# First loads and u products in a fixed order, first weights split on the chip, scores on two row halves, shorter inverse roots

## The chip, the cores and the metric

One core of a Trainium2 chip runs the kernel. The metric is the time of one execution on the device in microseconds (us), taken as the median of several runs. Engines: PE multiplies matrices, ACT applies functions and casts, DVE does arithmetic on tiles, POOL does simple arithmetic and issues some DMAs, SP only issues DMAs. Each engine works off its own instruction queue in order.

## The reference

A sequence of 512 rows of 1024 numbers passes two blocks. All in fp32:

```
# block 1
proj = rmsnorm(x) @ w_in                       # q, k, v, u, gates
o = softmax(q0 k0) v - lam softmax(q1 k1) v    # 8 heads, two 64-wide halves each, causal
s = s5_layer(u)                                # state space: tables from exp/sin/cos, a scan, gelu, glu
h = x + (g_attn * (o @ w_attn_proj) + g_ssm * (s @ w_ssm_proj)) @ w_out
h = h + (silu(conv gate) * conv val) @ w_down  # from rmsnorm(h) @ w_up
# block 2
m = [dilated_attention(8 heads of 64), rg_lru(...)] @ w_out_2
x = h + rms_norm(m);  x = x + rms_norm(relu(rms_norm(x) @ w_ff_in_2)^2 @ w_ff_out_2)
```

## The kernel before, in words

**Products.** Every fp32 operand a is split into hi, a rounded copy, and lo = a - hi. A product is three matmuls: hi by hi, hi by lo, lo by hi, all added up in PSUM (`mm3`). Activations are split by one cast on ACT and one subtraction on DVE (`split` of `Net`; tiles hi and lo, 128x512).

**Weights.** A `Unit` is a 512 KB piece of a weight matrix. `dma` issues its load into one of RB = 2 buffers raw (SP's queue). `split` casts raw to whi on ACT, writes wlo = -whi on ACT, and issues on POOL's queue a DMA that reads the weight from HBM a second time and adds it into wlo. There are WB = 4 buffers each of whi and wlo. After the split the unit gives raw back (`self.raw = None`). `drive` goes through the list of steps, and ahead of each it issues splits for units up to WB ahead and loads up to RB beyond that; `dma` returns at once if the unit holds a raw buffer.

**The order.** The program is a list of steps with costs. `merge` interleaves lists in proportion to cost. The build system then sets the order of instructions on each engine by readiness and program order, except where program order is kept by request.

**The front.** `front` loads cols (the small parameters), eight x tiles of 256 KB, two of the four u units (512 KB each), ident, pmask, and two spi tiles of 256 KB (the state space parameters), all on SP. For each x tile: hi and lo with the gain, then its square on ACT, and POOL adds the squares. `u_steps` multiplies x by the four u units into four PSUM banks, 96 matmuls of 128x512, position s by position s; `row1` sums the squares over the channels (tile rn, eight matmuls with one column) and takes the inverse root on DVE (`rsqrt`: 12 operations on a few columns). Beside it `ssm_steps` makes the tables of the state space: parameters (exp, sin; tiles sp, pw, rot), rotations ec and es (products by doubling, quarters 0 and 2 on one engine and the others on the other, POOL and DVE), and for each quarter Q the weights G, CL, L, whose products and transposes on PE (tile ps) give GT and K. Then U (u transposed), S = U by GT on PE, the scan on DVE, and xs, the states turned back, three operations on DVE and three on POOL. `gate_steps` multiply x by the gate units (PSUM tile cm, 24 matmuls a unit, then a product ga with R on DVE). `front2` loads the mask, the rope tables and gg (the head gains); POOL makes tab from rope and gg. `attention` joins these lists: u and two gate steps merged with the first part of the tables, then the rest.

**The attentions.** In the first attention a step of 64-row halves c = 0, 1 makes two score tiles s, each by three matmuls on 64 partitions, c = 0 first. In the second attention (`attn2_steps`) each step makes the scores of one head and one query tile (128, 256, 384 or 512 keys); heads 2j and 2j+1 lie on partitions 0 to 63 and 64 to 127 of the same tiles, and head 2j+1 comes four steps after head 2j's first. Following steps normalise (DVE), transpose (tile ta) and multiply with v (tile o).

Every engine call goes through a wrapper, so that nearly all instructions carry line 122; one goes by the names of the tiles.

Of the kernel before, what the change touches and what calls it, by code (L numbers as in the profile page):

```python
# [112 lines left out]
class Engine:  # L113


    def __init__(self, eng):
        self.eng = eng

    def __getattr__(self, name):
        f = getattr(self.eng, name)  # L120
        u = lambda a: a.ap if isinstance(a, V) else a
        return lambda *a, **k: f(*(u(x) for x in a), **{n: u(x) for n, x in k.items()})  # L122


class Core:
    def __init__(self, nc):
        for n in ("vector", "scalar", "gpsimd", "tensor", "sync"):
            setattr(self, n, Engine(getattr(nc, n)))


class Unit:


    def __init__(self, net, src, a, b):
        self.net, self.src, self.a, self.b = net, src, a, b
        self.pool = False
        self.raw = None
# [10 lines left out]
    def split(self):  # L148
        n = self.net
        w = self.a * self.b  # L150
        hi = n.wp.tile([128, 1024], F32R, tag="whi", bufs=n.WB, name=n.nm("whi"))
        lo = n.wp.tile([128, 1024], F32R, tag="wlo", bufs=n.WB, name=n.nm("wlo"))
        raw = self.raw[:, :w]
        n.nc.scalar.copy(out=hi[:, :w], in_=raw)
        n.nc.scalar.activation(out=lo[:, :w], in_=hi[:, :w].bitcast(F32), func=AF.Copy, scale=-1.0)
        self.raw = None
        self.hi = hi[:, :w].rearrange("p (a b) -> p a b", a=self.a)
        self.lo = lo[:, :w].rearrange("p (a b) -> p a b", a=self.a)

        n.nc.gpsimd.dma_start(out=self.lo, in_=self.src, accum_op=ADD)  # L160
# [23 lines left out]
class Net:  # L184
# [8 lines left out]
    def __init__(self, tc, ctx, ins, out):  # L193
        self.nc, self.I, self.out = Core(tc.nc), ins, out
# [80 lines left out]
    def front(self):  # L275
# [3 lines left out]
        self.u_units = [self.wunit("w_in_u", 0, 2 * u, 2) for u in range(4)]  # L279
        cols = self.c([128, NCOLS], "cols")  # L280
        Q.dma_start(out=cols, in_=I["cols"])
# [12 lines left out]
        self.ones1 = self.c([128, 128], "ones1")  # L294
        V.memset(self.ones1, 1.0)
        self.xg = []
        for k in range(8):
            x = self.t("x")
            Q.dma_start(out=x, in_=I["xT"][128 * k : 128 * k + 128, :])
            if k in (1, 3):  # L300
                self.u_units[k // 2].dma()
            self.xg.append(self.split(x, scale=self.cols["norm1_gain"][:, k : k + 1]))
            S.activation(out=x, in_=x, func=AF.Square)
            if k == 0:
                acc = x
            else:
                G.tensor_add(out=acc, in0=acc, in1=x)
        Q.dma_start(out=self.ident, in_=I["ident"])
        Q.dma_start(out=self.pmask, in_=I["pmask"])
        self.sp_in = [self.t("spi") for _ in range(2)]  # L310
        for i in range(2):
            Q.dma_start(out=self.sp_in[i], in_=I["ssmp"][:, 512 * i : 512 * i + 512])
        self.acc = {"x": acc}

    def row1(self):
# [3 lines left out]
        acc = self.acc.pop("x")  # L319
        ps = self.ps("rn")  # L320
        for j in range(8):
            a = acc[:, 128 * j : 128 * j + 128] if j < 4 else acc[:, j - 4 : 512 : 4]
            nc.tensor.matmul(ps[:, j : j + 1], a, self.onesd, start=True, stop=True)
# [9 lines left out]
        self.R1 = self.t("R1")  # L333
        S.copy(out=self.R1, in_=self.spread(rs))
# [35 lines left out]
    def rsqrt(self, out, x, w):  # L370

        V = self.nc.vector
        f, t, h = self.sm(w), self.sm(w), self.sm(w)
        V.tensor_copy(out=f, in_=x.bitcast(I32))
        V.tensor_scalar(out=f, in0=f, scalar1=-0.5, scalar2=1597463007.0, op0=MUL, op1=ADD)
        y = self.sm(w)
        V.tensor_copy(out=y.bitcast(I32), in_=f)

        V.tensor_mul(out=h, in0=y, in1=x)
        for i in range(2):  # L380
            V.scalar_tensor_tensor(out=t, in0=y, scalar=-0.5, in1=h, op0=MUL, op1=MUL)
            V.scalar_tensor_tensor(out=y, in0=t, scalar=1.5, in1=y, op0=ADD, op1=MUL)
            if i == 0:
                V.scalar_tensor_tensor(out=h, in0=t, scalar=1.5, in1=h, op0=ADD, op1=MUL)
        V.tensor_mul(out=h, in0=y, in1=x)
        V.scalar_tensor_tensor(out=t, in0=y, scalar=-0.5, in1=h, op0=MUL, op1=MUL)
        V.scalar_tensor_tensor(out=out, in0=t, scalar=1.5, in1=y, op0=ADD, op1=MUL)
# [50 lines left out]
    def qkv_steps(self, g):  # L438
# [4 lines left out]
        for kind, base in (("q", 0), ("k", 4), ("v", 8)):  # L443
            st = {"ps": [None, None], "y": [None, None]}
            units = [self.wunit("w_in_qkv", base + g, 4 * u, 4) for u in range(2)]
            for u, un in enumerate(units):
                un.pool = u == 0 or kind == "v"
# [98 lines left out]
    def attn_steps(self):  # L546
# [6 lines left out]
        def scores(u):  # L553
# [8 lines left out]
            mx = self.sm(2)  # L562
            for c in range(2):
                cs = slice(64 * c, 64 * c + 64)
                (qh, ql), (kh, kl) = grp["q"][hl], grp["k"][hl]
                ps = self.ps("s")
                self.mm3(ps[:, :n], (qh[cs, qs], ql[cs, qs]), (kh[cs, :n], kl[cs, :n]), True, True)
# [118 lines left out]
    def attention(self):  # L686
# [23 lines left out]
    def u_steps(self):  # L710
# [6 lines left out]
        for ui, un in enumerate(units):  # L717
            for b in range(2):
                def fn(ui=ui, un=un, b=b):
                    for s in (2 * b, 2 * b + 1):  # L720
                        if ui == 0:
                            st[s] = self.ps("u")
                        for kk in range(2):
                            k = 2 * ui + kk
                            xh, xl = self.xg[k]
                            sl = slice(s, 512, 4)
                            wh, wl = un.hi[:, kk, :], un.lo[:, kk, :]
                            mm = nc.tensor.matmul
                            mm(st[s], xh[:, sl], wh, start=k == 0, stop=False)
                            mm(st[s], xh[:, sl], wl, start=False, stop=False)  # L730
                            mm(st[s], xl[:, sl], wh, start=False, stop=k == 7)
                        if ui == 3:
                            if s == 0:
                                self.Z = [self.t("z") for _ in range(4)]
                            for q in range(4):
                                z = self.Z[q].rearrange("p (g s c) -> p g s c", g=8, s=4)[:, :, s, :]
                                src = st[s][:, q * 128 : q * 128 + 128].rearrange("p (g c) -> p g c", c=16)
                                S.activation(out=z, in_=src, func=AF.Copy, scale=self.rsp[:, s : s + 1])
                steps.append(Step(2.6, fn, un))
# [234 lines left out]
    def ssm_states(self, Q):  # L974
# [523 lines left out]
    def attn2_steps(self, q, k, att):  # L1498
# [3 lines left out]
        units = [(h, qt) for h in range(8) for qt in (3, 2, 1, 0)]  # L1502
        st = {}

        def scores(u):
            h, qt = u
            n = (qt + 1) * 128
            qs = slice(qt * 128, qt * 128 + 128)
            cs = slice(64 * (h % 2), 64 * (h % 2) + 64)
            (qh, ql), (kh, kl) = q[h // 2], k[h // 2]  # L1510
            ps = self.ps("s")
            self.mm3(ps[:, :n], (qh[cs, qs], ql[cs, qs]), (kh[cs, :n], kl[cs, :n]), True, True)
            e = self.t("e")
            mx, sm = self.sm(1), self.sm(1)
            V.tensor_tensor_reduce(out=e[:, :n], in0=ps[:, :n], in1=self.dmask[:, 512 - n :], scale=1.0,
# [4 lines left out]
            if h % 2 == 1 and qt == 0:  # L1520
                q[h // 2] = k[h // 2] = None
# [7 lines left out]
        def turn(u):  # L1529
# [7 lines left out]
            if qt % 2 == 1:  # L1537
                st["aT"] = [[self.tr("aT").rearrange("p (k q) -> p k q", k=2) for _ in range(2)] for _ in range(pr + 1)]
            for v in range(pr + 1):
                w = min(2, nk - 2 * v)  # L1540
                hi, lo = (a[:, :w, (qt % 2) * 128 : (qt % 2) * 128 + 128] for a in st["aT"][v])
                self.split(ps[:, 256 * v : 256 * v + w * 128].rearrange("p (k q) -> p k q", q=128), hi=hi, lo=lo)
            if qt % 2 == 0:
                st["pv", h, qt // 2] = st.pop("aT")
# [38 lines left out]
    def ffn2(self):  # L1583
# [29 lines left out]
        for f, un in first:  # L1613
            un.pool = True
# [152 lines left out]
```

## Time and profile before

| | us |
|---|---|
| median of 3 runs (1492.16 to 1494.91) | 1493.3 |
| profiled execution | 1495.94 |
| its span on the core | 1494.2 |
| PE busy | 1435.4 |
| DVE busy | 701.0 |
| ACT busy | 844.4 |
| POOL busy | 338.3 |

The span runs from the first to the last instruction. Busy times of PE are modelled ends of a pipeline: issue to issue is the better measure for one matmul. In the rows, "out<-in" names the tiles, and a bracket at the end of a row gives the idle time before it and what ended it.

### The profile page before, as it was taken

What the parts mean: (1) busy time and instruction counts of PE and PEld (TensorE: products, weight loads), DVE (VectorE), ACT (ScalarE), POOL (GpSimd) and SP (SyncE); (2) the same over time, 40 slices, a digit from 0 to 9 for tenths busy, and PEclk for the clock granted to TensorE, in tenths of its full rate; (3) what the DMA queues carried; (4) which work ended last, traced back from release to release, by engine and by line L of the source; (5) the groups of instructions that cost most, each with busy time, mean ns of one, the idle gap of its engine ahead of it and who ended that gap; (6) DMA issues with size and microseconds to landing.
All of it is one profiled execution on the core that took longest, in us unless ns stands there. A gap on an engine that the chain in (4) does not pass through costs nothing.

```text
span 1494.2 us, 20260 instructions
## 1 busy us (share of the span) xinstructions
PE 1435.4 (96%) x7448; PEld 1214.1 (81%) x7448; DVE 701.0 (47%) x1928; ACT 844.4 (57%) x1329; POOL 338.3 (23%) x450
## 2 busy tenths in 40 slices
PE   4898999999999999999999999999998999999997
PEld 4787898998888888888888887777887888888886
DVE  5977867877643345555541114565446111120003
ACT  6755466667544566666654445866556555454333
POOL 4763312212101211111121222103122111111110
PEclk9999999999999999999999999999999999999999
DMA  8564465555679878888889887756265888988994
GB/s 243 128 141 93 107 155 131 122 116 127 141 186 193 189 180 198 193 193 194 194 186 206 195 197 173 167 115 142 58 140 120 193 193 190 193 192 191 197 195 98
DMA packets 70451, 245.28 MB, mean 164 GB/s; under 512 B 8016, under 2 KB 8656, under 8 KB 70352
## 3 DMA queue, kind: packets, MB, share of 16 engines
q0 software_dynamic: 32912, 118.50, 48.4%
q1 hardware_dynamic: 36864, 124.43, 24.8%
q8 instruction: 59, 0.97, 0.3%
q10 hardware_dynamic: 576, 1.05, 0.2%
q14 instruction: 40, 0.33, 0.1%
HBM read 241.85 MB, written 2.10 MB: 163 GB/s over the span
## 4 chain that ended last, share of the span: by engine, by line
PE 78%; DVE 13%; ACT 3%; issue 2%; DMA 2%; POOL 1%; SPq 0%; DVEq 0%; ACTq 0%; POOLq 0%
PE cm L122 54%; PE ff L122 11%; PE pj L122 4%; DVE s L122 3%; PE s L122 2%; PE o L122 2%; PE v L122 1%; PE ta L122 1%; PE ps L122 1%; DVE e L122 1%; DVE v L122 1%; DVE lo L122 1%; DMA wlo<-in_w_ff_in_dram 1%; DVE oc L122 1%; ACT e L122 1%
## 5 line engine op out<-in xcount | busy, mean ns | idle before, releaser
L122 PE MATMUL cm<-hi,whi 128*128 128x512 f32 (+1 forms) x1328 | 513.1, 387 | 2.5 <-ACT hi L122 2.5
L122 PE MATMUL cm<-hi,wlo 128*128 128x512 f32 (+1 forms) x1328 | 509.7, 384 | 2.5 <-DMA wlo<-in_w_ff_in_dram 2.5
L122 PE MATMUL cm<-lo,whi 128*128 128x512 f32 (+1 forms) x1328 | 509.8, 384 | 2.2 <-DVE lo L122 2.1
L122 ACT CAST whi<-raw 128x1024 fp32r<-128x1024 f32 (+1 forms) x226 | 235.6, 1043 | 410.6 <-PE cm L122 320.8
L122 PEld LDWEIGHTS cm<-hi,wlo 128*128 128x128 f32 x1328 | 251.5, 189 | 51.5 <-ACT p L122 2.5
L122 PEld LDWEIGHTS cm<-lo,whi 128*128 128x128 f32 x1328 | 251.7, 190 | 51.0 <-DVE lo L122 3.7
L122 PEld LDWEIGHTS cm<-hi,whi 128*128 128x128 f32 x1328 | 251.3, 190 | 51.0 <-ACT hi L122 3.1
L122 ACT ACTIVATE wlo<-whi 128x1024 fp32r<-128x1024 f32 (+1 forms) x226 | 236.0, 1045 | 2.4
L122 PE MATMUL pj<-whi,hi 128*128 128x256 f32 x384 | 111.6, 291 | 0.0
L122 PE MATMUL pj<-wlo,hi 128*128 128x256 f32 x384 | 108.8, 283 | 0.0
L122 PE MATMUL pj<-whi,lo 128*128 128x256 f32 x384 | 108.7, 283 | 0.0
L122 PE MATMUL ff<-wlo,hi 128*128 128x512 f32 x256 | 99.7, 389 | 1.0 <-DMA wlo<-in_w_ff_out_dram 1.0
L122 PE MATMUL ff<-whi,hi 128*128 128x512 f32 x256 | 99.6, 389 | 0.0
L122 PE MATMUL ff<-whi,lo 128*128 128x512 f32 x256 | 99.6, 389 | 0.0
L122 DVE SCALAR_TENSOR_TENSOR y<-z,cols,y 128x511 f32<-128x511 f32 (+2 forms) x100 | 75.1, 751 | 46.1 <-ACT y L122 44.3
L122 POOL DMA_DIRECT2D wlo<-in_w_up_dram x44 | 37.8, 858 | 203.4 <-ACT wlo L122 203.4
L122 DVE SCALAR_TENSOR_TENSOR p<-cm,R 128x512 f32<-128x512 f32 (+1 forms) x35 | 22.2, 644 | 113.6 <-PE cm L122 112.3
L122 PEld LDWEIGHTS pj<-whi,hi 128*128 128x128 f32 x384 | 73.8, 192 | 0.9 <-issue 0.6
L122 PEld LDWEIGHTS pj<-wlo,hi 128*128 128x128 f32 x384 | 73.9, 192 | 0.1
L122 PEld LDWEIGHTS pj<-whi,lo 128*128 128x128 f32 x384 | 73.7, 192 | 0.0
L122 DVE TENSOR_TENSOR xT<-cm,xT 128x512 f32<-128x512 f32 x16 | 11.1, 692 | 118.7 <-PE cm L122 118.7
L122 POOL DMA_DIRECT2D wlo<-in_w_ff_in_dram x32 | 27.5, 858 | 158.7 <-ACT wlo L122 141.5
(298 smaller groups left out, 2112.2 us busy)
## 6 DMA issues: line engine op xcount, KB each, us to landing
raw<-in_w_up_dram SPq DMA_DIRECT2D x44, 512.0 KB, 3.6
wlo<-in_w_up_dram POOLq DMA_DIRECT2D x44, 512.0 KB, 5.5
raw<-in_w_ff_in_dram SPq DMA_DIRECT2D x32, 512.0 KB, 3.6
wlo<-in_w_ff_in_dram POOLq DMA_DIRECT2D x32, 512.0 KB, 5.7
raw<-in_w_ff_out_dram SPq DMA_DIRECT2D x32, 512.0 KB, 3.7
wlo<-in_w_ff_out_dram POOLq DMA_DIRECT2D x32, 512.0 KB, 5.7
raw<-in_w_in_qkv_dram SPq DMA_DIRECT2D x24, 512.0 KB, 3.7
wlo<-in_w_in_qkv_dram POOLq DMA_DIRECT2D x24, 512.0 KB, 6.9
```

The lines of the kernel that those rows point to most:

```text
L122: return lambda *a, **k: f(*(u(x) for x in a), **{n: u(x) for n, x in k.items()})
```

## The change

- The load of cols goes to ACT's queue. SP loads x and the u weights in another order; `front` itself issues all four u units' loads and splits, ahead of `drive`.
- u units (`un.dve`) get wlo = raw - whi by one DVE subtraction; no negation, no second read.
- `hold` keeps ACT (in `front`) and PE (to the end of u) in program order: all eight splits first, squares after; in u unit 0 all products with whi of a position come before those with wlo; the eight sums for rn are spread through unit 3's first half, `row1` follows there.
- Twelve matmuls on a zero tile and an early table load stand at the start.
- The first part of the tables is merged with four gate steps, after u instead of with u.
- The three xs operations of POOL go to DVE. The inverse root has 8 operations.
- Scores of two 64-row halves alternate matmul by matmul; in the second attention heads 2j and 2j+1 share a step.

```diff
 class Unit:
     def split(self):
+        if self.hi is not None:
+            return
...
         n.nc.scalar.copy(out=hi[:, :w], in_=raw)
-        n.nc.scalar.activation(out=lo[:, :w], in_=hi[:, :w].bitcast(F32), func=AF.Copy, scale=-1.0)
+        if self.dve:
+            n.nc.vector.tensor_sub(out=lo[:, :w], in0=raw, in1=hi[:, :w].bitcast(F32))
+        else:
+            n.nc.scalar.activation(out=lo[:, :w], in_=hi[:, :w].bitcast(F32), func=AF.Copy, scale=-1.0)
         self.raw = None
...
-        n.nc.gpsimd.dma_start(out=self.lo, in_=self.src, accum_op=ADD)
+        if not self.dve:
+
+            n.nc.gpsimd.dma_start(out=self.lo, in_=self.src, accum_op=ADD)
...
+    def mm3_halves(self, pairs):
+
+        mm = self.nc.tensor.matmul
+        for i, j in ((0, 0), (0, 1), (1, 0)):
+            for ps, a, b in pairs:
+                mm(ps, a[i], b[j], start=i + j == 0, stop=i == 1)
...
-        Q.dma_start(out=cols, in_=I["cols"])
+        S.dma_start(out=cols, in_=I["cols"])
...
+        w = self.ps("w0")[:, :128]
+        for j in range(12):
+            nc.tensor.matmul(w, z[:, :128], z[:, :128], start=j == 0, stop=j == 11)
...
+        nc.hold(True, "scalar", "tensor")
+        for k in range(8):
+            self.xg.append(self.split(xs[k], scale=self.cols["norm1_gain"][:, k : k + 1]))
+            if k in (0, 3):
+                u[k // 2].split()
+            if k == 3:
+                u[2].dma()
...
-        u.insert(4, Step(0, self.row1))
         rest.insert(2, Step(1, self.front2))
-        steps = merge(u + ga[:2], first)
-        steps += merge(ga[2:] + self.qkv_steps(0), rest + self.glu_steps())
+        steps = u + merge(ga[:4], first)
+        steps += merge(ga[4:] + self.qkv_steps(0), rest + self.glu_steps())
...
-        G.tensor_mul(out=sh(xs[1]), in0=on(ri), in1=on(ec))
-        G.tensor_mul(out=on(b), in0=on(rr), in1=on(es))
-        G.tensor_add(out=sh(xs[1]), in0=sh(xs[1]), in1=on(b))
+        V.tensor_mul(out=sh(xs[1]), in0=on(ri), in1=on(ec))
+        V.tensor_mul(out=on(b), in0=on(rr), in1=on(es))
+        V.tensor_add(out=sh(xs[1]), in0=sh(xs[1]), in1=on(b))
...
-        units = [(h, qt) for h in range(8) for qt in (3, 2, 1, 0)]
+
+        units = [(2 * j + i, qt) for j in range(4) for qt in (3, 2, 1, 0) for i in range(2)]
```

The queue of SP before, from the third u load on; raw is a weight's buffer, spi, dB, cmask, rope and gg are small inputs:

```order
L122 DMA raw_33_167<-in_w_in_u_dram 128x1024
L122 DMA dB_66_347<-in_ssm_d_dram 128x512
L122 DMA cmask_158_877<-in_cmask_dram 128x512
L122 DMA rope_159_879<-in_ropec_dram 128x256
L122 DMA raw_36_174<-in_w_in_u_dram 128x1024
L122 DMA rope_159_879<-in_ropes_dram 128x256
L122 DMA raw_39_181<-in_w_in_g_dram 128x1024
L122 DMA gg_160_882<-in_rows_dram 128x384
```

The same place in the queue of SP after the change, from the fourth u load on:

```order
L124 DMA raw_36_160<-in_w_in_u_dram 128x1024
L124 DMA dB_96_532<-in_ssm_d_dram 128x512
L124 DMA cmask_173_960<-in_cmask_dram 128x512
L124 DMA raw_41_191<-in_w_in_u_dram 128x1024
L124 DMA rope_174_962<-in_ropec_dram 128x256
L124 DMA rope_174_962<-in_ropes_dram 128x256
L124 DMA raw_42_193<-in_w_in_u_dram 128x1024
L124 DMA raw_43_195<-in_w_in_u_dram 128x1024
L124 DMA raw_44_197<-in_w_in_u_dram 128x1024
L124 DMA raw_45_199<-in_w_in_g_dram 128x1024
L124 DMA gg_175_965<-in_rows_dram 128x384
```

Four more loads of u weights (raw_41 to raw_44) stand ahead of the first gate weight and of gg: `drive` calls `dma` of the u units, whose raw is None again after their splits.

The queue of POOL before, from the last sum of squares on; wlo<-in_w_in_g is the adding DMA of a gate weight:

```order
L122 TENSOR_TENSOR x_1_78<-x_1_78,x_24_137 128x512
L122 DMA wlo_32_163<-in_w_in_u_dram 128x1024
L122 DMA wlo_35_170<-in_w_in_u_dram 128x1024
L122 DMA wlo_38_177<-in_w_in_u_dram 128x1024
L122 TENSOR_TENSOR tab_161_884<-rope_159_879,gg_160_882 128x256
L122 TENSOR_TENSOR tab_161_884<-rope_159_879,gg_160_882 128x4x32 x2
L122 DMA wlo_72_372<-in_w_in_g_dram 128x1024
```

The same place in the queue of POOL after the change; rot, ec, es and tm belong to the rotations:

```order
L124 TENSOR_TENSOR x_3_92<-x_3_92,x_12_110 128x512
L124 TENSOR_TENSOR tm_128_703<-es_127_702,rot_95_497 128x4
...
L124 TENSOR_TENSOR tab_176_967<-rope_174_962,gg_175_965 128x256
L124 TENSOR_TENSOR tab_176_967<-rope_174_962,gg_175_965 128x4x32 x2
L124 TENSOR_TENSOR tab_177_971<-rope_174_962,gg_175_965 128x256
...
L124 TENSOR_TENSOR tab_177_971<-rope_174_962,gg_175_965 128x4x32
L124 TENSOR_TENSOR ec_126_701<-ec_126_701,tm_128_703 128x4x2
L124 TENSOR_TENSOR tab_177_971<-rope_174_962,gg_175_965 128x4x32
L124 DMA wlo_52_232<-in_w_in_g_dram 128x1024
```

The first adding DMA of a gate weight, behind three tab operations before, stands behind rotations of the first quarter and all six tab operations.

PE before, the first scores of the second attention (hi and lo of q, then of k):

```order
L122 MATMUL s_1715_9332<-hi_1645_8982,hi_1628_8922 128x512
L122 MATMUL s_1715_9332<-lo_1646_8983,hi_1628_8922 128x512
L122 MATMUL s_1715_9332<-hi_1645_8982,lo_1629_8923 128x512
L122 MATMUL s_1719_9342<-hi_1645_8982,hi_1628_8922 128x384
L122 MATMUL s_1719_9342<-lo_1646_8983,hi_1628_8922 128x384
```

PE after the change, the same place:

```order
L124 MATMUL s_1702_9255<-hi_1632_8905,hi_1615_8845 128x512
L124 MATMUL s_1703_9256<-hi_1632_8905,hi_1615_8845 128x512
L124 MATMUL s_1702_9255<-lo_1633_8906,hi_1615_8845 128x512
L124 MATMUL s_1703_9256<-lo_1633_8906,hi_1615_8845 128x512
L124 MATMUL s_1702_9255<-hi_1632_8905,lo_1616_8846 128x512
L124 MATMUL s_1703_9256<-hi_1632_8905,lo_1616_8846 128x512
```

Before, one head's tile of 512 keys is followed by the same head's tile of 384; now two heads' tiles of 512 (s_1702, s_1703) alternate. For the last pair of heads (8 of 32 groups of three) the order keeps each head's three matmuls mostly together.

## Rows read from the trace of the kernel before

**Rows 1.** The page's head and first part: busy us, share, instructions.
```profile
span 1494.2 us, 20260 instructions
PE 1435.4 (96%) x7448; PEld 1214.1 (81%) x7448; DVE 701.0 (47%) x1928; ACT 844.4 (57%) x1329; POOL 338.3 (23%) x450
```

**Rows 2.** Waits of PE: for what, us in total, times, longest.
```profile
PE u L122 <- DMA wlo<-in_w_in_u_dram: 10.4, 2, 9.1
PE u L122 <- ACT whi L122: 9.0, 1, 9.0
PE S L122 <- ACT U L122: 7.6, 2, 7.4
PE ps L122 <- ACT CL L122: 5.3, 1, 5.3
```

**Rows 3.** Stretches: length, busy us by engine (instructions), clock, DMA share, GB/s.
```profile
0.00:202.70 202.70, 165.06 (x976) 148.98 (x976) 157.28 (x474) 121.63 (x206) 98.48 (x158) 0.95 0.60 142
0.00:10.00 10.00, 1.00 (x2) 0.87 (x3) 3.65 (x25) 4.72 (x7) 0.34 (x6) 1.00 0.80 260
10.00:20.00 10.00, 1.09 (x3) 0.33 (x1) 6.75 (x5) 7.58 (x13) 8.47 (x7) 1.00 0.98 280
1000.00:1050.00 50.00, 49.87 (x265) 39.65 (x263) 31.69 (x114) 32.20 (x78) 15.15 (x15) 1.00 0.61 133
```

**Rows 4.** Timeline of PE in the front: start, us, instruction, idle before.
```profile
49.94 0.40 PE L122 MATMUL u<-wlo,hi 128*128 128x512 f32 x1
50.17 0.39 PE L122 MATMUL u<-whi,lo 128*128 128x512 f32 x1
...
85.22 2.02 PE L122 MATMUL S<-U,GT 128*128 128x128 f32 x16
```

**Rows 5.** Timeline of POOL in the front.
```profile
33.77 1.64 POOL L122 TENSOR_TENSOR tab<-rope,gg 128x256 f32<-128x256 f32 x3 [4.36 <-DMA gg<-in_rows_dram]
...
44.92 1.12 POOL L122 TENSOR_TENSOR tab<-rope,gg 128x256 f32<-128x256 f32 x1 [2.96 <-DVE rot L122]
...
85.58 0.73 POOL L122 TENSOR_TENSOR es<-es,tm 128x256 f32<-128x256 f32 x1
```

**Rows 6.** DMA issues, 0 to 140 us: count, size, median us to landing.
```profile
raw<-in_w_in_g_dram SPq DMA_DIRECT2D x8, 512.0 KB, 4.8
wlo<-in_w_in_g_dram POOLq DMA_DIRECT2D x8, 512.0 KB, 5.7
...
gg<-in_rows_dram SPq DMA_DIRECT2D x1, 192.0 KB, 8.9
```

**Rows 7.** Timeline of DVE in the front.
```profile
44.77 0.16 DVE L122 TENSOR_SCALAR rot<-sp 128x16 f32<-128x16 f32 x1
...
86.99 1.28 DVE L122 TENSOR_TENSOR v<-S,es 128x512 f32<-128x512 f32 x2
...
92.53 1.71 DVE L122 TENSOR_TENSOR xs<-rr,ec 128x508 f32<-128x508 f32 x1
```

**Rows 8.** Timeline of ACT: the sine of the parameters.
```profile
29.57 0.32 ACT L122 ACTIVATE sp<-sp 128x16 f32<-128x16 f32 x2
```

**Rows 9.** Timeline of PE: scores of the first attention.
```profile
202.78 0.53 PE L122 MATMUL s<-hi,hi 64*128 64x512 f32 x2
...
203.71 0.39 PE L122 MATMUL pj<-whi,hi 128*128 128x256 f32 x1
```

**Rows 10.** Timeline of PE: scores of the second attention, one head at a time.
```profile
987.41 0.32 PE L122 MATMUL s<-hi,hi 64*128 64x128 f32 x1
...
987.89 0.66 PE L122 MATMUL ta<-ident,e 128*128 128x128 f32 x4
988.47 0.50 PE L122 MATMUL s<-hi,hi 64*128 64x512 f32 x1
...
989.37 0.55 PE L122 MATMUL ta<-ident,e 128*128 128x128 f32 x3
```

**Rows 11.** Timeline of DVE: an inverse root in a row norm.
```profile
1106.11 0.82 DVE L122 SCALAR_TENSOR_TENSOR s<-s,s 128x2 f32<-128x2 f32 x5
```

More of the change, by code (lines that the diff above doesn't have):

```diff
@@ L113, with __init__ @@
 class Engine:
-    def __init__(self, eng):
-        self.eng = eng
+    def __init__(self, eng, tc):
+        self.eng, self.tc, self.held = eng, tc, False
     def __getattr__(self, name):
@@ L121, in __getattr__, with call, __init__, hold @@
         u = lambda a: a.ap if isinstance(a, V) else a
-        return lambda *a, **k: f(*(u(x) for x in a), **{n: u(x) for n, x in k.items()})
+        def call(*a, **k):
+            r = f(*(u(x) for x in a), **{n: u(x) for n, x in k.items()})
+            return self.tc.keep_in_program_order(r) if self.held else r
+        return call
 class Core:
-    def __init__(self, nc):
+    def __init__(self, tc):
         for n in ("vector", "scalar", "gpsimd", "tensor", "sync"):
-            setattr(self, n, Engine(getattr(nc, n)))
+            setattr(self, n, Engine(getattr(tc.nc, n), tc))
+    def hold(self, on, *names):
+        for n in names:
+            getattr(self, n).held = on
 class Unit:
@@ L135, in __init__ @@
         self.net, self.src, self.a, self.b = net, src, a, b
-        self.pool = False
-        self.raw = None
+        self.dve = False
+        self.raw = self.hi = None
     def dma(self):
@@ L193, in __init__ @@
     def __init__(self, tc, ctx, ins, out):
-        self.nc, self.I, self.out = Core(tc.nc), ins, out
+        self.nc, self.I, self.out = Core(tc), ins, out
         P = lambda name, **k: ctx.enter_context(tc.tile_pool(name=name, **k))
@@ L279, in front @@
         self.u_units = [self.wunit("w_in_u", 0, 2 * u, 2) for u in range(4)]
+        for un in self.u_units:
+            un.dve = True
         cols = self.c([128, NCOLS], "cols")
-        Q.dma_start(out=cols, in_=I["cols"])
+        S.dma_start(out=cols, in_=I["cols"])
         self.cols, at = {}, 0
@@ L293, in front @@
         V.memset(self.onesd, 1.0 / D)
-        self.ones1 = self.c([128, 128], "ones1")
-        V.memset(self.ones1, 1.0)
-        self.xg = []
+        z = self.t("z0")
+        G.memset(z, 0.0)
+        w = self.ps("w0")[:, :128]
+        for j in range(12):
+            nc.tensor.matmul(w, z[:, :128], z[:, :128], start=j == 0, stop=j == 11)
+        S.activation(out=z[:, 0:1], in_=self.onesd, func=AF.Square)
+        self.xg, xs, u = [], [], self.u_units
         for k in range(8):
@@ L299, in front @@
             Q.dma_start(out=x, in_=I["xT"][128 * k : 128 * k + 128, :])
[L300 to L307, printed above, removed]
+            xs.append(x)
+            if k in (0, 3):
+                u[k // 2].dma()
         Q.dma_start(out=self.ident, in_=I["ident"])
         Q.dma_start(out=self.pmask, in_=I["pmask"])
+        nc.hold(True, "scalar", "tensor")
+        for k in range(8):
+            self.xg.append(self.split(xs[k], scale=self.cols["norm1_gain"][:, k : k + 1]))
+            if k in (0, 3):
+                u[k // 2].split()
+            if k == 3:
+                u[2].dma()
         self.sp_in = [self.t("spi") for _ in range(2)]
@@ L312, in front, with row1_sum @@
             Q.dma_start(out=self.sp_in[i], in_=I["ssmp"][:, 512 * i : 512 * i + 512])
-        self.acc = {"x": acc}
+        u[3].dma()
+        acc = xs[0]
+        for k, x in enumerate(xs):
+            S.activation(out=x, in_=x, func=AF.Square)
+            if k:
+                G.tensor_add(out=acc, in0=acc, in1=x)
+            if k == 3:
+                u[2].split()
+        u[3].split()
+        nc.hold(False, "scalar")
+        self.acc = {"x": acc}
+    def row1_sum(self, j):
+        if j == 0:
+            self.rn = self.ps("rn")
+        acc = self.acc["x"]
+        a = acc[:, 128 * j : 128 * j + 128] if j < 4 else acc[:, j - 4 : 512 : 4]
+        self.nc.tensor.matmul(self.rn[:, j : j + 1], a, self.onesd, start=True, stop=True)
     def row1(self):
@@ L318, in row1 @@
         V, S = nc.vector, nc.scalar
[L319 to L323, printed above, removed]
+        del self.acc["x"]
+        ps = self.rn
+        self.rn = None
         rs = self.c([128, 8], "rs1")
@@ L372, in rsqrt @@
         V = self.nc.vector
[L373 to L377, printed above, removed]
-        V.tensor_mul(out=h, in0=y, in1=x)
[L380 to L387, printed above, removed]
+        h, t, y = self.sm(w), self.sm(w), self.sm(w)
+        stt = V.scalar_tensor_tensor
+        V.tensor_scalar(out=y.bitcast(I32), in0=x.bitcast(I32), scalar1=-0.5, scalar2=1595932665.0, op0=MUL, op1=ADD)
+        V.tensor_mul(out=h, in0=y, in1=x)
+        stt(out=t, in0=y, scalar=-0.703952253, in1=h, op0=MUL, op1=MUL)
+        stt(out=y, in0=t, scalar=0.703952253 * 2.38924456, in1=y, op0=ADD, op1=MUL)
+        c = math.sqrt(0.375)
+        stt(out=h, in0=y, scalar=c, in1=x, op0=MUL, op1=MUL)
+        V.tensor_mul(out=h, in0=h, in1=y)
+        stt(out=t, in0=h, scalar=-1.25 / c, in1=h, op0=ADD, op1=MUL)
+        stt(out=out, in0=t, scalar=1.875, in1=y, op0=ADD, op1=MUL)
     def rsqrt_act(self, out, x, w):
@@ L562, in scores @@
             mx = self.sm(2)
+            (qh, ql), (kh, kl) = grp["q"][hl], grp["k"][hl]
+            two = []
             for c in range(2):
                 cs = slice(64 * c, 64 * c + 64)
-                (qh, ql), (kh, kl) = grp["q"][hl], grp["k"][hl]
-                ps = self.ps("s")
-                self.mm3(ps[:, :n], (qh[cs, qs], ql[cs, qs]), (kh[cs, :n], kl[cs, :n]), True, True)
+                two.append((self.ps("s")[:, :n], (qh[cs, qs], ql[cs, qs]), (kh[cs, :n], kl[cs, :n])))
+            self.mm3_halves(two)
+            for c in range(2):
+                ps = two[c][0]
                 e = self.t("e")
@@ L719, in fn @@
                 def fn(ui=ui, un=un, b=b):
-                    for s in (2 * b, 2 * b + 1):
-                        if ui == 0:
-                            st[s] = self.ps("u")
[L723 to L734, printed above, removed]
+                    todo = ([(0, k, s) for k in (0, 1) for s in range(4)] if ui == 0 and b == 0 else
+                            [(p, k, s) for p in (1, 2) for k in (0, 1) for s in range(4)] if ui == 0 else
+                            [(p, k, s) for s in (2 * b, 2 * b + 1) for k in (0, 1) for p in range(3)])
+                    for p, kk, s in todo:
+                        k = 2 * ui + kk
+                        if ui == 0 and b == 0 and kk == 0:
+                            st[s] = self.ps("u")
+                        x, w = ((self.xg[k][0], un.hi), (self.xg[k][0], un.lo), (self.xg[k][1], un.hi))[p]
+                        nc.tensor.matmul(st[s], x[:, s:512:4], w[:, kk, :], start=k == 0 and p == 0, stop=k == 7 and p == 2)
+                        if ui == 3 and b == 0 and p > 0:
+                            self.row1_sum(4 * s + 2 * kk + p - 1)
+                    if ui == 3 and b == 0:
+                        self.row1()
+                    if ui == 3 and b == 1:
+                        nc.hold(False, "tensor")
+                        self.Z = [self.t("z") for _ in range(4)]
+                        for s in range(4):
                             for q in range(4):
@@ L738, in fn @@
                                 S.activation(out=z, in_=src, func=AF.Copy, scale=self.rsp[:, s : s + 1])
+                        self.R1 = self.t("R1")
+                        S.copy(out=self.R1, in_=self.spread(self.rs))
                 steps.append(Step(2.6, fn, un))
@@ L1507, in scores @@
             n = (qt + 1) * 128
[L1508 to L1512, printed above, removed]
+            if h % 2 == 0:
+                qs = slice(qt * 128, qt * 128 + 128)
+                (qh, ql), (kh, kl) = q[h // 2], k[h // 2]
+                two = []
+                for cs in (slice(0, 64), slice(64, 128)):
+                    two.append((self.ps("s")[:, :n], (qh[cs, qs], ql[cs, qs]), (kh[cs, :n], kl[cs, :n])))
+                self.mm3_halves(two)
+                st["s"] = [x[0] for x in two]
+            ps = st["s"][h % 2]
             e = self.t("e")
             mx, sm = self.sm(1), self.sm(1)
-            V.tensor_tensor_reduce(out=e[:, :n], in0=ps[:, :n], in1=self.dmask[:, 512 - n :], scale=1.0,
+            V.tensor_tensor_reduce(out=e[:, :n], in0=ps, in1=self.dmask[:, 512 - n :], scale=1.0,
                                    scalar=NEG, op0=ADD, op1=MAX, accum_out=mx)
@@ L1519, in scores @@
             st[u] = (e, sm)
-            if h % 2 == 1 and qt == 0:
-                q[h // 2] = k[h // 2] = None
+            if h % 2 == 1:
+                del st["s"]
+                if qt == 0:
+                    q[h // 2] = k[h // 2] = None
         def combine(u):
@@ L1612, in ffn2 @@
         first = [(f, self.wunit("w_ff_in_2", f, 0, 8)) for f in range(self.HB)]
-        for f, un in first:
-            un.pool = True
         fps = {}
```

10 lines of the change are left out of this document (3 added, 7 removed).

## Prediction

> **What bounds the kernel now.** I read the page's first part, the engine's list of waits, the stretches, and then the timelines of the front. PE is busy for 1435.4 of 1494.2 us [rows 1], so a saving counts only where PE stands idle or where its own work shrinks. The waits say where it stands idle: 9.0 us until the first cast of a u weight, 10.4 us on the DMAs that finish the low halves of the u weights, 5.3 us on CL and 7.6 us on U, both before the first scores [rows 2]. Everything else on the list is 2.5 us or less. Up to the first scores at 202.78 us PE is busy for 165.06 us [rows 3]: 37.6 us of idleness in the front, of the 58.8 us in the whole span (1494.2 less 1435.4). Later it is packed: 49.87 of 50 us in the second attention [rows 3]. So the change can pay in two places, the front (by at most 37.6 us and what the clock gives back) and the score products.
>
> **The u products.** At present they start at 9.0 us, wait again for 9.1 us [rows 2] and end at about 50.4 (the last issue at 50.17 plus one pitch of 0.23 us) [rows 4]. The change puts the first u weight second in SP's queue instead of fourth, and its low half no longer takes a cast, a negation on ACT and an accumulating DMA but a cast and one DVE subtraction. No subtraction of 1024 columns stands in the trace; from below two DVE operations of 508 columns (an xs product, 1.71 us beside POOL work [rows 7]) make 3.4 us an upper price, and 0.64 us for each 512 columns where POOL rests (two of 1.28 us in all, [rows 7]) makes 1.3 us a lower one. I take 2. What paces the products then is the arrival of the weights: x, the four u weights and the spi tiles are 4.5 MB; at the 260 and 280 GB/s of the first two stretches [rows 3] they have moved by 17 us, and as the last weight waits for a raw buffer, I put it at 20. Its cast and subtraction, behind DVE's and ACT's work on x, end at about 24, its 24 matmuls take 5.6 us, and behind the units before them I get the end of u at 34: 16 us earlier.
>
> **What takes most of it back.** The next PE work is three gate units. Their first two products per unit need only the cast half; then the first unit needs wlo_232, and PE's queue is in order. Two queues hold wlo_232 up. On SP, four further loads of u weights now stand ahead of the first gate weight (the order of SP shows them: the loop that issues ahead asks a u unit for its load again once its raw buffer was given back). Nothing reads them, but they pass through the two raw buffers, a pair at a time; two pairs at 4.8 us a load [rows 6] are some 10 us, so the gate weight is issued near 29, lands near 34, and its cast and negation end near 37. On POOL the accumulating DMA stands behind six rotation operations, which need rot, and five tab operations, which need gg. rot was written at 44.77, 15 us after the sine at 29.57 [rows 7, 8]; the tables' chain starts some 6 us earlier now, so 38. gg is issued right behind the gate weight and takes 8.9 us [rows 6]: 38 as well. In the trace the first three tab operations took 1.64 us and the next 1.12 [rows 5]; with the small ones I count 5 to 6 us. So the DMA goes out at 44 and lands 5.7 us later [rows 6], at 50. Between 34 and 50 PE has only six matmuls, 1.4 us: 14.6 of the 16 us go into a new wait.
>
> **What is kept.** From 50 PE runs 120 gate matmuls before the first S product, where before it had run 77 by 85.22 [rows 4]. In my walk along the two orders that S still comes at about 85, since the tables on DVE set it, but 43 matmuls more lie behind it: 43 x 0.23 = 9.9 us of work done in what were waits. The wait on U, 7.4 us at its longest [rows 2], shrinks by some 4, because POOL no longer runs the three xs products between the rotations (DVE's six at an undisturbed 0.64 each are 3.8 us, where at present its three, of 1.71 us for the first [rows 7], cost no less), though wlo_695 behind the rotations of the next quarter (until 85.58 plus 0.73 [rows 5]) gives PE a new stop of about 5, which the 43 matmuls already paid for. Front: 14 us. Bounds: 30 if of the 37.6 us idle only some 8, a little under the present 9.0 of the first weight, remain; on the other side a loss of 10, if the 7.5 us of the useless loads (2 MB at 280 GB/s) and a later gg move the tables and nothing covers it.
>
> **Scores in the first attention: nothing.** The diff alternates the two 64-row halves. The trace shows them side by side already: at 202.78 two hi,hi products of 64x512 begin together, and all six are through 0.93 us later (203.71) [rows 9], while three of one head took 0.90 us alone (988.47 to 989.37) [rows 10]. The Trainium skill states the opposite ("TensorE: Matmul & The Clock Gate", Part 3, what overlaps): matmuls start and end in strict program order. By that rule the halves, which stand one after the other in the order of before, ran in series, and alternating them would spare 32 times some 0.69 us, 22 us. The trace disagrees: six in 0.93 us. The 22 us are a rival below.
>
> **Scores in the second attention.** There the two heads of a pair stood in different steps, so each ran alone: 0.90 us for 512 columns, 0.48 for 128 (987.41 to 987.89) [rows 10], 0.69 in the mean of the four sizes if the two between lie on the line. Each pair now costs what one head cost: 16 pairs, of which PE's order alternates 12; the last four stand head after head, partly apart. 12 x 0.69 = 8.3 us; bounds 3 (the stretch of the last heads may wait for DVE and ACT) and 11 (all 16).
>
> **Shorter inverse roots.** Four of 12 DVE operations go; a chained one costs 0.17 us (five in 0.82) [rows 11]. That is 0.7 us for a chain. Those inside the attentions lie beside matmuls of other steps, so they count nothing; two row norms at the block ends have PE waiting: 1.5 us, bounds 0 and 3. The table loads, the tanh, the warm-up matmuls and the early memset lie before the first weight has landed: nothing there, and if the twelve matmuls delayed the first product it would be by under 1 us of a queue that then waits for weights anyway. The attributes named pool were read by nothing.
>
> **The sum** against the profiled execution: 14 + 8.3 + 1.5 = 23.8, so a span of 1470.4 for 1494.2, 1472.1 with the 1.7 us around it; the median of the runs lies 2.6 us below that execution: 1469.5, say 1470.
>
> **Rivals.**
> (a) The new wait is short: gg and rot are there before the gate weight's halves, the DMA goes out at 37 and PE stops for 8 us instead of 15; and the second stop of 5 us, behind the rotations of the next quarter, moves out of PE's way with it. For it: rot's chain is short operations only. Against it: gg, 8.9 us [rows 6] behind that weight. The 12 us join the front: 1458.
> (b) The wait eats the whole front. The tables, not PE, set the first scores: DVE must still do the same chain, and in the order of DVE a gate evacuation that needs wlo_232 stands ahead of the second quarter's tables. Then the extra gate matmuls only move waits about. Front 2 us: 1482. For it: the 5.3 and 7.4 us waits of now are both on such tables [rows 2].
> (c) Slower: that evacuation holds DVE. If wlo_232 lands not at 50 but after 74, it moves the tables of the second quarter, the scans and the first scores by more than the 24 us forecast here; each further microsecond is lost in full. At 82 (POOL's rotations, of both quarters, done only at 86 now [rows 5]) the front loses 18 and the total is 1501. Against it: POOL's order puts only six rotation operations ahead.
> (d) Front as forecast, but in the second attention DVE and ACT set the pace, so the paired products only wait: 1478.
> (e) The rule of strict order holds and the first attention gains too: 1448. The page is "TensorE: Matmul & The Clock Gate". Against it: the rows quoted.
>
> **How the numbers follow.** Forecast 0.38, (a) 0.20, (b) 0.22, (c) 0.09, (d) 0.09, (e) 0.02. The forecast's own range is 1463 to 1477. For 8 in 10 the range takes in (a), (d) and most of (b), down to 1456 and up to 1488. About 0.2%, 3 us, is what a measurement can tell from no change. Nearly all of (a), (b), (d) and the forecast lie below 1490: faster 0.87; same 0.05, from the far end of (b); slower 0.08, from (c).
>
> **What would show it.** In the profile after: last u matmul near 34; PE's wait on the DMA of a gate wlo of about 14 us; four loads of u weights more than now; the first scores near 188; six score products of two heads in 0.9 us after 950 and the pairs of the first attention as long as now. I am wrong if no gate wait shows, if the first scores come after 200, or if the first attention's scores get shorter.

## The result and the profile after

The changed kernel takes 1476.22 us (median of 4 runs, 1475.57 to 1478.87) against 1494.11: ratio 0.9885, 95% interval 0.9868 to 0.9902, some 17 us faster. The forecast was 1470 in a range from 1456 to 1488. The profiled execution took 1476.77 us with a span of 1474.8, 19.4 less than the span before. The page's head and first part after, answering to [rows 1]:

```profile
span 1474.8 us, 20214 instructions
PE 1428.8 (97%) x7472; PEld 1211.2 (82%) x7472; DVE 681.7 (46%) x1851; ACT 839.5 (57%) x1326; POOL 316.4 (21%) x435
```

The waits of PE after (what for, us in total, times, longest), answering to [rows 2]:

```profile
PE cm L124 <- DMA wlo<-in_w_ff_in_dram: 6.4, 2, 4.3
PE cm L124 <- DMA wlo<-in_w_in_g_dram: 6.1, 1, 6.1
PE cm L124 <- ACT whi L124: 3.8, 2, 2.4
PE u L124 <- DVE wlo L124: 3.1, 1, 3.1
PE S L124 <- ACT U L124: 2.6, 1, 2.6
PE o L124 <- ACT aT L124: 2.0, 3, 1.0
PE u L124 <- ACT whi L124: 1.9, 1, 1.9
PE ta L124 <- DVE e L124: 1.4, 1, 1.4
```

The waits of u, CL and U are gone or short; new are the gate weights (cm on wlo of in_w_in_g, and on whi) and, in the second attention, ta and o. The longest, on wlo of in_w_ff_in (2.5 us before), lies in block 2 behind the attentions. The front in the timelines after, first SP, then POOL, then PE (start, us, instruction, idle before):

```profile
24.14 0.33 SPq L124 DMA_DIRECT2D raw<-in_w_in_u_dram  x1
...
27.36 4.13 SPq L124 DMA_DIRECT2D raw<-in_w_in_u_dram  x3
33.31 0.33 SPq L124 DMA_DIRECT2D raw<-in_w_in_g_dram  x1
37.37 0.33 SPq L124 DMA_DIRECT2D gg<-in_rows_dram  x1
```

```profile
40.34 0.49 POOL L124 TENSOR_TENSOR tm<-es,rot 128x4 f32<-128x4 f32 x1 [15.09 <-DVE rot L124]
...
42.29 2.27 POOL L124 TENSOR_TENSOR tab<-rope,gg 128x256 f32<-128x256 f32 x4
...
46.05 1.00 POOL L124 DMA_DIRECT2D wlo<-in_w_in_g_dram  x1
```

```profile
24.17 0.63 PE L124 MATMUL u<-wlo,hi 128*128 128x512 f32 x1 [3.10 <-DVE wlo L124]
...
40.01 0.39 PE L124 MATMUL u<-whi,lo 128*128 128x512 f32 x1
...
46.95 0.63 PE L124 MATMUL cm<-lo,whi 128*128 128x512 f32 x1
53.64 0.80 PE L124 MATMUL cm<-hi,wlo 128*128 128x512 f32 x1 [6.06 <-DMA wlo<-in_w_in_g_dram]
...
88.50 0.39 PE L124 MATMUL cm<-hi,wlo 128*128 128x512 f32 x1
88.73 1.95 PE L124 MATMUL S<-U,GT 128*128 128x128 f32 x16
```

DVE in the same stretch:

```profile
61.56 0.69 DVE L124 TENSOR_TENSOR ga<-cm,R 128x512 f32<-128x512 f32 x1 [7.05 <-PE cm L124]
```

The four useless loads are issued from 24.14 on, the gate weight at 33.31; POOL starts its rotations at 40.34, the adding DMA goes out at 46.05, PE goes on at 53.64. DVE stands idle for 7.05 us until PE has the first gate product, and the first S follows directly behind gate matmuls.

Where the 19.4 us of the two profiled spans came from, read at the same instructions in PE's timelines (us from the span's start):

| | before | after | gained so far |
|---|---|---|---|
| first scores | 202.8 | 188.8 | 14.0 |
| last o of the first attention | 431.7 | 415.2 | 16.5 |
| last v of block 2 | 957.5 | 940.6 | 16.9 |
| last o of the second attention | 1067.6 | 1048.6 | 19.0 |
| end of the span | 1494.2 | 1474.8 | 19.4 |

The execution profiled before began its products at 9.0 us and its scores at 202.8. Those of b_att2 and b_half1, whose front is that of before, began at 8.1 and 7.9 and had their first scores at 201.2 and 201.5, so 1.3 to 1.6 of the 14.0 is that execution.

### The profile page after: what moved, and what is told of

Same layout as the page of the kernel before. It is cut to its first block, busy times and chain, and to the rows that moved or that the text cites. A ratio compares the mean times of both kernels' runs of the same rounds, so it can differ in the third digit from the quotient of the medians.

```text
span 1474.8 us, 20214 instructions
## 1 busy us (share of the span) xinstructions
PE 1428.8 (97%) x7472; PEld 1211.2 (82%) x7472; DVE 681.7 (46%) x1851; ACT 839.5 (57%) x1326; POOL 316.4 (21%) x435
## 5 line engine op out<-in xcount | busy, mean ns | idle before, releaser
L124 ACT ACTIVATE wlo<-whi 128x1024 fp32r<-128x1024 f32 (+1 forms) x222 | 231.9, 1045 | 2.3
L124 DVE TENSOR_TENSOR z<-cm,R 128x512 f32<-128x512 f32 x48 | 33.2, 691 | 58.4 <-PE cm L124 54.6
```

The costliest lines, as they stand in the source:

```text
L124: r = f(*(u(x) for x in a), **{n: u(x) for n, x in k.items()})
```

## The experiments

All ratios are to the kernel before on the same chip. Single runs of the kernel before lie within 5 us of their median, those of kernels with the pairs at their first depth up to 7. For the changed kernel the ratio is 0.9885, 0.9868 to 0.9902. A difference between two of the rows below carries the noise of both.

| | us | ratio, 95% |
|---|---|---|
| before, second attention paired (b_att2) | 1493.2 | 1.0003, 0.9989 to 1.0018 |
| before, shorter roots (b_rsqrt) | 1486.2 | 0.9945, 0.9933 to 0.9957 |
| before, first attention alternated (b_half1) | 1491.0 | 0.9979, 0.9971 to 0.9988 |
| before, U's copy listed earlier (b_chk) | 1491.3 | 0.9983, 0.9974 to 0.9991 |
| after, no useless loads (a_nodup) | 1476.6 | 0.9885, 0.9866 to 0.9904 |
| after, long roots (a_rsqrtold) | 1478.2 | 0.9901, 0.9884 to 0.9919 |
| after, xs on POOL again (a_xspool) | 1480.8 | 0.9913, 0.9900 to 0.9927 |
| after, second attention as before (a_att2old) | 1477.6 | 0.9901, 0.9885 to 0.9916 |
| after, two gate steps (a_ga2dup) | 1471.0 | 0.9858, 0.9842 to 0.9873 |
| after, two gate steps, no useless loads (a_ga2) | 1470.0 | 0.9833, 0.9817 to 0.9849 |
| after, later transposes (a_deep) | 1471.1 | 0.9848, 0.9835 to 0.9861 |
| a_ga2 and a_deep together (best) | 1464.8 | 0.9810, 0.9794 to 0.9826 |

**The useless loads (a_nodup).**

```diff
     def dma(self):
-        if self.raw is not None:
+        if self.raw is not None or self.hi is not None:
             return
```

> The changed kernel without the four useless loads of u weights (a unit that is split returns from its load at once). On POOL the adding DMAs of the first three gate weights then stand ahead of the rotations and tab operations. Theory: the useless loads and the place of the DMA on POOL are what PE waits for between 41 and 54 us (2.8, 1.8 and 6.7 us from issue to issue, and half clock behind them); without them the gate weight is issued near 24 instead of 33 us, its low half lands before 40, these waits go, the first scores come at 176 to 181 instead of 188.8 and the time is 1464 to 1469 us. Rival: the tables on DVE set the first scores, PE waits a little later for them instead, and the time stays within 2 us of 1476.

The rival's time held, but not its reason: PE waited later not for the tables but again for a gate weight. The first gate weight was issued at 24.79 and the first three adding DMAs from 31.96 on, and PE did not stop between 41 and 54. It stopped later and longer, for the fourth gate weight, whose DMA POOL reached only behind its rotations. PE, then POOL:

```profile
61.03 0.40 PE L124 MATMUL cm<-lo,whi 128*128 128x512 f32 x1
74.49 0.80 PE L124 MATMUL cm<-hi,wlo 128*128 128x512 f32 x1 [13.07 <-DMA wlo<-in_w_in_g_dram]
```

```profile
69.14 0.88 POOL L124 DMA_DIRECT2D wlo<-in_w_in_g_dram  x1
```

The first S (89.7) and the first scores (188.7) came when they had come before. A wait taken away ahead of another wait gave nothing.

**Fewer gate steps beside the tables (a_ga2, a_ga2dup).**

```diff
-        steps = u + merge(ga[:4], first)
-        steps += merge(ga[4:] + self.qkv_steps(0), rest + self.glu_steps())
+        steps = u + merge(ga[:2], first)
+        steps += merge(ga[2:] + self.qkv_steps(0), rest + self.glu_steps())
```

> The changed kernel without the useless loads and with two gate steps instead of four beside the first tables. Theory: the four gate steps put up to 120 gate matmuls, and the waits for their wlo, ahead of the first S product in PE's order, so that DVE idles between 60 and 100 us; with two steps the first S comes at 76 to 82 us instead of 88.7, the first scores at 181 to 185, the time is 1468 to 1472 us. Rival: DVE is the bound from 100 us on and has the same sum to do; first scores near 188, time 1475 to 1477.

> The changed kernel with two gate steps instead of four beside the first tables, but with the four useless loads. In POOL's order the adding DMA of the first gate weight stands behind rotations and tab operations, as in the changed kernel. Theory: without the wait for that DMA at the start of the gate steps the front gains, so here, where it is back, PE stops for 5 to 8 us again and the first S comes near 85; time 1472 to 1476. Rival: the useless loads cost nothing in this order either, 1470 as without them.

The last gate matmul and the first S of a_ga2:

```profile
76.89 0.39 PE L124 MATMUL cm<-lo,whi 128*128 128x512 f32 x1
77.11 1.95 PE L124 MATMUL S<-U,GT 128*128 128x128 f32 x16
```

The first theory held. Of the second the wait came back, but the time, 1471.0, lies below its range. With two steps the fourth gate weight no longer stands ahead of the first S, which came at 77.1 (82.9 with the useless loads); the first scores at 181.7 (186.0). In a_ga2 PE waits for no gate weight at all; in a_ga2dup it waits 10.6 us for one. The medians of the two differ by 1 us and the ratios by 0.0025, 3.7 us, with overlapping intervals, so what the useless loads cost here is not settled; beside four gate steps they cost nothing (a_nodup). Two gate steps instead of four gave 0.0027, 4 us, with the useless loads kept (each run of a_ga2dup is below each of the changed kernel) and 0.0052, 7.8 us, without them: in the front the four gate steps are the larger cost. The tables' own work allows an S at 77.1; in the changed kernel and in a_nodup the gate steps, with their waits, hold it up to 88.7 and 89.7.

**The xs operations (a_xspool)**, three of them on POOL as in the diff's removed lines.

> The changed kernel with three of the six xs operations of each quarter back on POOL, as before the change. Forecast: moving them to DVE freed POOL and made the wait for U shrink by some 4 us; undoing it brings 3 to 5 us back (1479 to 1481). Theory after the other runs: that wait goes by the order on ACT; with three operations on each engine, slowed by each other, DVE is busy about as long as with six alone, and the time stays within 2 us of 1476.

The forecast held: 0.0028 or 4 us, first scores at 193.9 instead of 188.8. PE's wait for U is 5.2 us instead of 2.6, and another, of tile Y for DVE's lo, 3.6 instead of 0.7; so the wait for U is about half of the 5.2 us by which the first scores come later. DVE after, for one quarter, and in a_xspool:

```profile
96.33 0.66 DVE L124 TENSOR_TENSOR xs<-rr,ec 128x508 f32<-128x508 f32 x1
96.91 0.68 DVE L124 TENSOR_TENSOR v<-ri,es 128x508 f32<-128x508 f32 x1
97.51 0.68 DVE L124 TENSOR_TENSOR xs<-ri,ec 128x508 f32<-128x508 f32 x1
```

```profile
95.60 1.71 DVE L124 TENSOR_TENSOR xs<-rr,ec 128x508 f32<-128x508 f32 x1
97.23 1.76 DVE L124 TENSOR_TENSOR v<-ri,es 128x508 f32<-128x508 f32 x1
```

**The roots (b_rsqrt, a_rsqrtold) and the place of U (b_chk).** The diff of the roots is part of the change; b_chk moves one step:

```diff
-        rest = [..., wts(2), rot(3), tab(3), chk(2), sta(2), ...]
+        rest = [..., wts(2), rot(3), chk(2), tab(3), sta(2), ...]
```

> The kernel before with the shorter inverse root alone. Forecast term: 1.5 us less, all of it behind 1100 us at the row norms. Theory after the result: 2 to 3 us less, most of it already by the end of the first attention, where waits for the inverse roots of q and k (1.3 us for tq) and for DVE (1.0 us) shrank.

> The changed kernel with the longer inverse root of before. Alone on the kernel before the shorter one gave 8.2 us, 5 to 7 of it in the front, where ACT's copy of U for the third quarter came to stand ahead of the CL and H casts instead of behind them. Theory: that part is a matter of the order on ACT and DVE, which the rest of the change settles anyway; undoing the shorter root costs only its direct part, 1 to 3 us (1477 to 1479). Rival: it is the root itself, and undoing it costs 8 us (1484).

> The kernel before with one step moved and nothing else: the transposes and the copy of U of the third quarter are listed ahead of the tables of the fourth. Theory: the 7.4 us wait for U is U's copy standing in ACT's queue behind CL and H, which wait for DVE; with the copy ahead the wait shrinks to some 3 us and the time falls by 4 to 6 us (1488 to 1490). Rival: DVE's load sets the third S product whatever the order, and nothing changes.

Alone the roots gave 8.2 us, against 1.5 forecast and 2 to 3 expected. Their first scores came at 194.0, those of b_half1, whose front is that of before, at 201.5: 7.5 us lie in the front, 5.4 of them already at the third S (122.1 against 127.5), ahead of which only one root is taken, four operations shorter. ACT's queue shows what else differs. In b_half1, then in b_rsqrt:

```profile
125.32 0.89 ACT L122 ACTIVATE CL<-oc,pmask 128x256 f32<-128x256 f32 x2
126.11 0.89 ACT L122 ACTIVATE H<-oc,pmask 128x256 f32<-128x256 f32 x2
126.91 0.56 ACT L122 COPY U<-U 128x512 f32<-128x512 f32 x1
```

```profile
121.48 0.59 ACT L122 COPY U<-U 128x512 f32<-128x512 f32 x1
...
123.44 0.91 ACT L122 ACTIVATE CL<-oc,pmask 128x256 f32<-128x256 f32 x2
```

With the shorter root as the only edit, the build system put U's copy ahead of CL and H; PE's wait for U fell from 7.4 to 4.1 us. b_chk, which only lists that copy earlier, gave 2.5 us where 4 to 6 were expected, its wait for U 4.8: the order is a cause, but not the whole 7.5, and what makes up the rest was not separated. In the changed kernel, undoing the roots cost 0.0016, 2 us, as expected, though not clear of the noise. It excludes the 8 us of the rival; that the other parts had settled the order is argued, not shown.

**The first attention (b_half1).**

> The kernel before with the scores of the first attention alone alternated between the two row halves. Forecast: nothing (within 0.5 us), since the halves already run side by side. Rival by the rule of strict program order: 22 us less.

3.1 us, neither. The 32 groups of score products took 23.6 us in the trace before and 22.9 in b_half1, so they ran side by side already (in 30 groups; in two, other products stand between the halves in both kernels), and the 22 us are not to be had. What else shrank is waits: tq for s, then s for aT, 1.62, 0.84 and 0.73 us from issue to issue before, none over 0.6 in b_half1.

**The second attention (b_att2, a_att2old, a_deep).** b_att2 and a_att2old exchange `attn2_steps` whole; a_deep:

```diff
-        ot, op = 3, 5
+        ot, op = 5, 7
```

> The kernel before with one part of the change alone: in the second attention heads 2j and 2j+1 share a step and their score products alternate. Forecast term: 8.3 us less (1485.8). Theory after the result: PE's own work shrinks by some 8 us but the two units of a step reach DVE and ACT together, and PE waits for them; 2 to 3 us less (1491 to 1492).

> The changed kernel with the second attention as before the change (one head a step, three matmuls in a row). Theory: paired at a depth of 3 and 5 steps it gains nothing to speak of, since what PE saves comes back as waits and half clock: the time is 1475 to 1478 us, like the changed kernel, the stretch from the last v product to the last product o 107 to 110 us. Rival (forecast): undoing it costs 8 us (1484).

> The changed kernel with the second attention's transposes two steps later and its products with v two steps later as well (3 and 5 steps behind the scores become 5 and 7). Theory: since two units share a step, PE reaches their transposes before DVE has normalised them and waits some 5 us in all; two steps more take these waits away and with them the falls of the clock, 3 to 5 us less (1471 to 1473). Rival: the waits come from buffers or from DVE's load, and nothing is gained.

Pairing alone gave nothing (1.0003, where 2 to 3 us were expected), and undoing it in the changed kernel cost 2.4 us, not clear of the noise: the forecast term of 8.3 fell. The stretch from the last v to the last o, before and after (length, then busy us of PE, weight loads, DVE, ACT, POOL, clock):

```profile
957.50:1068.00 110.50, 110.16 (x567) 87.96 (x567) 71.41 (x259) 71.19 (x175) 20.83 (x21) 0.97 0.52 114
```

```profile
940.60:1049.00 108.40, 102.75 (x574) 82.76 (x573) 70.61 (x259) 69.70 (x175) 20.90 (x21) 0.97 0.53 116
```

PE's work shrank by 7.4 us, its idleness grew from 0.3 to 5.7. Both stretches hold 6.8 us at half clock. At full clock throughout, unpaired (b_rsqrt) and paired (a_nodup), they differ by 2.6 us:

```profile
947.90:1055.80 107.90, 107.27 (x566) 84.90 (x565) 71.18 (x259) 71.06 (x174) 20.84 (x21) 1.00 0.53 117
```

```profile
940.60:1045.90 105.30, 99.64 (x573) 80.53 (x572) 70.60 (x259) 69.81 (x175) 20.98 (x21) 1.00 0.54 120
```

One such wait after, behind a pair of scores:

```profile
969.80 0.40 PE L124 MATMUL s<-hi,lo 64*128 64x512 f32 x2
971.21 0.41 PE L124 MATMUL ta<-ident,e 128*128 128x128 f32 x2 [1.00 <-DVE aT L124]
```

The clock adds to it. The stretch's last 41 us in b_att2, and 33 in a_nodup, which has the same pairs:

```profile
1029.00:1049.00 20.00, 18.61 (x95) 14.54 (x94) 13.60 (x54) 13.34 (x36) 5.49 (x5) 0.81 0.57 120
1049.00:1070.00 21.00, 20.95 (x102) 18.77 (x101) 12.75 (x55) 9.24 (x32) 1.29 (x1) 0.62 0.00 1
```

```profile
1013.00:1033.00 20.00, 18.16 (x117) 14.59 (x115) 16.60 (x70) 16.26 (x45) 5.50 (x5) 1.00 0.56 126
1033.00:1046.00 13.00, 12.00 (x85) 10.35 (x83) 9.62 (x40) 6.90 (x26) 1.28 (x1) 1.00 0.00 1
```

With the same pairs the clock stayed at full in one execution and fell in the other, and the whole stretch took 105.0 (a_nodup) or 113.7 us (b_att2). PE had the same wait in both, in b_att2 1.7 us before the clock fell:

```profile
1039.54 0.44 PE L122 MATMUL ta<-ident,e 128*128 128x128 f32 x2 [1.39 <-DVE e L122]
```

```profile
1023.91 0.44 PE L124 MATMUL ta<-ident,e 128*128 128x128 f32 x2 [1.39 <-DVE e L124]
```

In six of the seven profiles with the pairs at this depth the clock fell 1 to 2 us behind that wait, for 3.4 to 23.9 us; in a_nodup it did not. The 12 runs of b_att2 lie in two groups, 1489.9 to 1494.3 us (mean granted clock 0.982 to 0.986) and 1497.3 to 1499.8 (0.979 to 0.980). With later transposes (a_deep) that wait is 1.0 us, the stretch took 103.1 us at full clock and the time fell by 0.0037, 5 us:

```profile
940.70:1044.00 103.30, 99.52 (x575) 80.27 (x574) 70.78 (x259) 69.57 (x174) 21.34 (x21) 1.00 0.55 122
```

PE is idle for 3.8 us there instead of 5.7; the rest of what the stretch gained is clock. In best, with the same depth, it stayed at full too.

**Together (best).**

> The changed kernel without the useless loads, with two gate steps beside the first tables, and with the second attention's later steps put off by two. Theory: the gains of the two experiments lie in different stretches and add: some 6 us in the front and 2 to 5 in the second attention, 1464 to 1467 us. Rival: one of them is eaten again by what follows, 1470.

1464.8 us: the two gains add, nearly (7.8 and 5.5 us alone, 11 together), 28 us under the kernel before.

## Why the prediction was right, and where its steps were not

The sum held, at 23.8 forecast and 17 to 19 measured. In part that was luck: the front came out at its size by another way than the one worked out, and the errors behind it partly cancelled.

- End of u: forecast 34, measured 40.2. The arrival of the weights was to pace the products. Instead the third unit, cast on ACT at 14.83 us, got its subtraction at 22.90, behind DVE's small operations on the parameters, six of which took some 1.3 us instead of 0.16 while POOL added the squares. PE waited 3.1 us for it; half clock behind that cost about 1.7 and the norm sums between unit 3's products about 3.2.
- The new wait: cause right, size not. The adding DMA went out behind the rotations and the tab operations at 46.05 instead of 44, and PE resumed at 53.64 instead of 50. But as u ended later, PE stood idle for 9.8 us (6.1 on the DMA, 3.8 on two casts), not 14.6. The half clock behind it, with a matmul every 0.43 us instead of 0.23 until 59, is not in the sum.
- First S 88.7 for 85, first scores 188.8 for 188: the numbers came, the reason failed. It was to be the tables on DVE that set S, with 43 more gate matmuls done for nothing in what were waits. But with two gate steps S came at 77.1 and the first scores 7 us earlier (a_ga2): the gate steps ahead of S held it up, in PE's order and through DVE, idle for 7.05 us until the first gate product.
- Rivals (b) and (c) had seen that this gate product stands in DVE's order ahead of the tables. Their size was wrong: (b) let the front gain 2 us, (c) lose 18, and it gained 12 to 14.
- The shrinking wait for U: 7.4 to 2.6, as forecast, and POOL's xs operations are a cause (it is 5.2 in a_xspool). That the order on ACT sets it as well was not seen.
- A stop of 5 us at wlo_695: not in the list of waits.
- "Each pair now costs what one head cost" was right for PE; that this shortens the stretch was the step that failed behind the front (2 us for 8.3). Rival (d) had it, the steps behind a pair come too early for DVE and ACT, and its 1478 is nearer to the measured 1476 than the forecast's 1470. The row that PE is full in 1000 to 1050 [rows 3] says only what PE does now, not what is next in line.
- Shorter roots: 1.5 forecast, at the row norms behind the attentions. No gain shows there: from the last o to the end the profiles have 426.6 us before, 426.2 after and 426.0 in a_rsqrtold. Alone they gave 8.2, most of it in the front, and in the changed kernel some 2.
- First attention: 0 forecast, 2.5 measured, as vanished waits. Rival (e) is out by b_half1.

## What to carry to other kernels

When one queue wait is removed, follow the same engine's order to the next operand that stands behind the same queue before counting the gain: taking out the useless loads alone gave nothing, fewer gate steps ahead of the first S gave 4 us alone, and both together 7.8. Work spared on the busiest engine can come back as waits for those that feed it (here 7.4 us spared, 2 gained): try the dependent steps further behind in the same edit. Where a build system orders the queues, a small edit far away may reorder them, so time each part alone and in place.

## What was not expected of the hardware

Behind one and the same wait of 1.39 us in an otherwise busy PE, the granted clock fell to half in six profiles, for 3.4, 6.8 or 23.9 us, and in a seventh not at all; for the stretch that is a difference of up to 8.7 us (105.0 against 113.7). Such a wait is not needed either: in the kernel before the clock fell at 1058.9 us, where PE had been busy for 19.66 of the last 20. What decides it is not shown. DVE's products of 508 columns took 0.66 to 0.68 us alone and 1.71 to 1.76 beside POOL's, so in the changed kernel's first quarter six on DVE (4.1 us) are faster than three on DVE beside three on POOL (4.6).
